# The seven products of w_out: one weight sum on VectorE, another order of the products, gated transfers of x, factors made earlier

## The chip, the cores and the metric

The kernel runs on one core of a Trainium2 chip. Its engines are TensorE (PE; its weight loads are shown as PEld), VectorE (DVE), ScalarE (ACT), GpSimd (POOL) and SyncE (SP); each works through its own instructions in order, and they meet through semaphores. SP and POOL also issue transfers (DMA) between the chip's main memory (DRAM) and the on-chip memory (SBUF); all transfers share the core's 16 DMA engines. The metric is the device time of one execution in microseconds.

## What is computed

One layer of a hybrid encoder over 512 tokens and 2048 features. After the input projection, attention and the gating unit, two branches are merged, projected by `w_out` and added to `x`; then comes a squared-ReLU MLP:

```python
merged = jax.nn.sigmoid(gate_a) * y_a + jax.nn.sigmoid(gate_b) * y_b
x = x + merged @ w_out[l]

h2 = rms_norm(x, g_ff[l])
x = x + jnp.square(jax.nn.relu(h2 @ w_ff1[l])) @ w_ff2[l]
```

The change concerns `x + merged @ w_out[l]`: 512 x 2048 times 2048 x 2048, in float32.

## The kernel before

**Exact products from split factors.** PE multiplies a rounded float32 form, so each factor is split: `hi` is the rounded copy (made on ACT, line 113) and `lo` the rest (made on DVE, line 114). One product then takes three matmuls (`mm3`, lines 72 to 74): hi x hi, hi x lo, lo x hi.

**Seven products instead of eight.** The large projections use Strassen's scheme in Winograd's form: a 2 x 2 block product with seven block multiplications, named y11, y21, m7, m6, y22, m4 and m5. Each needs a weight factor (a weight block or a sum of blocks) and an activation factor. Class `Sums` (line 168) makes the weight factors of one 2 x 2 set of blocks, w11, w12, w21, w22, in six tiles of 128 x 1024 numbers (512 KB): four for the blocks, one (`a`) for m7's factor, one (`c`) for m6's and then y22's. `Sums.loads` gives SP the loads; `Sums.parts(name)` makes the sum that the product needs and splits it into hi and lo. In w_out the sums are made in two ways:

- by a transfer that adds to what is in SBUF (issued by POOL, `accum_op=ALU.add`): m7's factor (`given`: `a` is loaded with one block by SP and the other is added by line 321), m5's (line 192, issued at m7), y22's (line 205, issued right after m6's factor has been split: block (1, 0) is added to `c`);
- by an addition on DVE: m6's (line 194).

**The stage of w_out.** Lines 940 to 966 call `strassen_tokens` four times: `f` is the half of the 2048 rows of `w_out`, `g` the half of its columns, in the order (0, 0), (0, 1), (1, 0), (1, 1). A call makes two `Sums` (`i`, each of 4 x 128 rows) and then, product by product, multiplies: 2 `Sums` x 2 token tiles x 2 row blocks x 3 = 24 matmuls of 128 x 512. The order of the products is `NAMES` (line 159), and another one in the last call (`last`, line 324). When a product is done, `evac_x` adds it from PSUM to the result tiles `x2[token tile, column block]`; `takes` (line 901) says to which and with what sign, and `done` (line 904) with which product a tile is complete. Complete tiles are written to DRAM (`kept`, line 952), squared for the next norm and scaled (lines 954 and 955).

**x itself** is added by transfers too: in the calls (0, 1) and (1, 0), `between_x` (line 957) issues after each product one or two accumulating transfers (256 KB, on POOL) into the `x2` tiles of the other column half. Their only condition is that the tile's own last addition is done.

**The activation factors** are kept in `ms`: `split_merged` makes y11, y21 and y22, `merged_factors` makes m7, m6, m4 and m5, each with a subtraction or an addition on DVE (line 255), a copy on ACT and a subtraction on DVE. For the row half `f` = 0 they are indices 0 to 3, for `f` = 1 indices 4 to 7. When they are made is written out by hand: `steps` (lines 828 to 870) is a list of tasks by step, where a step is a piece of a projection (in w_oa and w_ob) or a product (in w_out); step `OB` = 16 is the first of w_ob, `XO` = 32 the first product of w_out, `FF` = 60 the first piece of the MLP.

**What sets the order.** The instructions of an engine are put in order when the kernel is built, by a planner that goes by dependencies, by the order in the program and by a simulation of times; an instruction can stand in its queue ahead of another that the program names first. `tc.issue_after(ins)` puts the issues in its block behind `ins` on that engine. Tiles come from pools: `slots` has 64 tiles of 128 x 512, the weight tiles two pools of six, the split weights (`w_piece`) six, which is three pairs of hi and lo. A tile that is asked for again waits for its last reader.

Of the kernel before, what the change touches and what calls it, by code (L numbers as in the profile page):

```python
# [13 lines left out]
ALU = mybir.AluOpType  # L14
AX = mybir.AxisListType

P = 128
# [11 lines left out]
W = 512  # L29
# [6 lines left out]
def tile_hybrid_layer(ctx: ExitStack, tc: tile.TileContext, x, g_mix, w_in, g_q, g_k, ln_g, ln_b,  # L36
# [4 lines left out]
    nc = tc.nc  # L41
# [21 lines left out]
    def tiny(n, name):  # L63
        return small.tile([P, n], F32, name=name, tag=f"tiny{n}")
# [103 lines left out]
    class Sums:  # L168


        def __init__(self, blocks, tiles, loaded=True, twice=False, given=False):


            self.blocks, self.loaded, self.twice, self.given = blocks, loaded, twice, given
            self.w11, self.w12, self.w21, self.w22, self.a, self.c = tiles
            self.take = {"y11": self.w11, "y21": self.w12, "m7": self.a, "m6": self.c, "y22": self.c,
                         "m4": self.w22, "m5": self.w21}

        def loads(self):
            order = [(self.w11, (0, 0)), (self.w12, (1, 0)), (self.w21, (0, 1)), (self.w22, (1, 1))]  # L180
            if self.given:
                order.insert(2, (self.a, (0, 0)))
            for t, hc in order:
                self.load = state["load"] = nc.sync.dma_start(out=t, in_=self.blocks[hc])
                yield

        def parts(self, name):
            if name == "m7":
                if not self.given:
                    nc.vector.tensor_tensor(out=self.a, in0=self.w11, in1=self.w21, op=ALU.add)  # L190
                if self.loaded:
                    state["sum"] = nc.gpsimd.dma_start(out=self.w21, in_=self.blocks[1, 1], accum_op=ALU.add)  # L192
            if name == "m6":
                nc.vector.tensor_tensor(out=self.c, in0=self.a, in1=self.w22, op=ALU.add)  # L194
            if name == "y22" and not self.twice:
                nc.vector.tensor_tensor(out=self.c, in0=self.c, in1=self.w12, op=ALU.add)
            if name == "m5" and not self.loaded:
                nc.vector.tensor_tensor(out=self.w21, in0=self.w21, in1=self.w22, op=ALU.add)
            src = self.take[name]
            hi, lo = piece("w_hi"), piece("w_lo")  # L200
            like = "p (k c) -> p k c"
            hi, lo = (t.rearrange(like, k=src.shape[1]) for t in (hi, lo))
            split_to(hi, lo, src)
            if name == "m6" and self.twice:
                state["sum"] = nc.gpsimd.dma_start(out=self.c, in_=self.blocks[1, 0], accum_op=ALU.add)
            return hi, lo
# [97 lines left out]

    SIGNS = (1.0, -1.0)

    def strassen_tokens(wap, r0, c0, lhs, evac, between, loaded=True, after=None, last=False, by_dma=False):

        KQ = 2
        ws = []  # L310
        for i in range(2):
            rows = wap[r0 + i * 2 * KQ * P:r0 + (i + 1) * 2 * KQ * P, :]
            blocks = {(h, c): rows[:, c0 + c * W:c0 + (c + 1) * W].rearrange("(k h p) c -> h p k c", p=P, h=2)[h]
                      for h in range(2) for c in range(2)}
            pool = (state["raw"], state["more"])[i]
            ws.append(Sums(blocks, [pool.tile([P, KQ, W], F32, name="w_raw", tag="w_raw") for _ in range(6)],
                           loaded, by_dma, by_dma))
        collections.deque(zip(*[w.loads() for w in ws]), 0)
        if by_dma:
            for w in ws:  # L320
                nc.gpsimd.dma_start(out=w.a, in_=w.blocks[0, 1], accum_op=ALU.add)
        state["loads"] = [w.load for w in ws]
        banks = {}
        names = ("y11", "m7", "m6", "m5", "y22", "m4", "y21") if last else NAMES
        for name in names:
            b, new = BANK[name]
            if new:
                banks[b] = [(aux if b in (1, 3) else acc)("q") for _ in range(2)]
            factors = []
            turns = [(i, t) for i in range(2) for t in range(2)]  # L330
            if last and name == names[-1]:
                turns.sort(key=lambda it: it[1])
            for i, t in turns:
                if i == len(factors):
                    with tc.issue_after(after.ins) if after and name == "m7" else nullcontext():
                        factors.append(ws[i].parts(name))
                hi, lo = factors[i]
                for k in range(KQ):
                    y = [part[:, t * P:(t + 1) * P] for part in lhs[name][i * KQ + k]]
                    mm3(banks[b][t], y, (hi[:, k, :], lo[:, k, :]), new and i == 0 and k == 0,  # L340
                        i == 1 and k == KQ - 1, skip_group_check=True)
            for t in range(2):
                evac(name, t, banks[b][t])
            between(name)
            step()
# [26 lines left out]
    mhalf = const.tile([P, 4], F32, name="mhalf")  # L372
# [258 lines left out]
    wsT, ws, bs = [], [], []  # L631
# [61 lines left out]
    for half in range(2):  # L693
# [4 lines left out]
        if half:  # L698
            steps = collections.defaultdict(list)
# [52 lines left out]
    order = gate_pairs[:1]  # L752
# [10 lines left out]
    for i, item in enumerate(order):  # L763
# [6 lines left out]
        else:  # L770
            c0, n, func = item
# [56 lines left out]
    steps = collections.defaultdict(list)  # L828
# [10 lines left out]
    def split_merged(k, names=("y11", "y21", "y22")):  # L839
        for name in names:  # L840
            half = int(name[2]) - 1
            ms[name, k] = halves(mt[2 * k + int(name[1]) - 1][:, half * HS:(half + 1) * HS])

    def merged_factors(k, *names):
        for name in names:
            factor(ms, mt[2 * k:2 * k + 2], k, name)

    OB, XO, FF = 16, 32, 60
    for i in range(2):
        n, a, b = OB + 4 * (i + 1), 2 * i, 2 * i + 1  # L850
        for at, f in enumerate([lambda a=a: split_merged(a),
# [1 line left out]
                                lambda a=a, b=b: (merged_factors(a, "m4", "m5"), merged_factors(b, "m7")),  # L853
                                lambda b=b: merged_factors(b, "m6", "m4", "m5")]):
            steps[n + at].append(f)
    for i in range(2):
        steps[OB + 14 + i].append(lambda i=i: split_merged(4 + i, ("y11", "y21")))
    steps[XO].append(lambda: [split_merged(4 + i, ("y22",)) for i in range(2)])
    for i in range(2):
        steps[XO + 1 + i].append(lambda i=i: split_merged(6 + i))  # L860
        for n, name in ((7, "m6"), (10, "m4"), (15, "m5")):
            steps[XO + n + i].append(lambda i=i, name=name: [merged_factors(4 + 2 * i + c, name) for c in range(2)])
    for i in range(4):
        steps[XO + 3 + i].append(lambda i=i: merged_factors(4 + i, "m7"))
    for n, what in ((21, (0, 0)), (22, (0, 1)), (23, (1, 0)), (24, (1, 1)), (25, (3, 1)), (26, (2, 1)), (27, (3, 0)),
                    (27, (2, 0))):
        steps[XO + n].append(lambda what=what: turned(*what))
# [29 lines left out]
    x2, x2T, hs = {}, {}, {}  # L897
# [29 lines left out]
            factor(hs, act, k, name, -1.0 if name in ("m7", "m4") else None, pool)  # L927

    CHUNK = 4

    class Merged:

# [7 lines left out]
    for f in range(2):  # L940
        for g in range(2):
            def evac_x(name, t, o):
                for half, c, op in takes[name]:
                    key = 2 * half + t, 2 * g + c
                    if key not in x2:
                        x2[key] = slot("x2")
                        nc.scalar.activation(out=x2[key], in_=o, func=AF.Copy, scale=1.0 if op == ALU.add else -1.0)
                    else:
                        nc.vector.tensor_tensor(out=x2[key], in0=x2[key], in1=o, op=op)
                for half, c in done[g].get(name, []) if f else []:  # L950
                    tb, j = 2 * half + t, 2 * g + c
                    nc.sync.dma_start(out=kept[tb, j], in_=x2[tb, j])
                    xs = x2s[tb, j] = slot("xs")
                    nc.scalar.activation(out=xs, in_=x2[tb, j], func=AF.Square, accum_out=ss2[:, tb, j:j + 1])
                    nc.scalar.activation(out=xs, in_=x2[tb, j], func=AF.Copy, scale=rstd[:, tb:tb + 1])

            def between_x(name):
                if f != g:
                    i = NAMES.index(name)
                    for n in (i, len(NAMES)) if i == len(NAMES) - 1 else (i,):  # L960
                        tb, j = n % NTB, 2 * (1 - g) + n // NTB
                        nc.gpsimd.dma_start(out=x2[tb, j], in_=x[tb * P:(tb + 1) * P, j * W:(j + 1) * W],
                                            accum_op=ALU.add)

            strassen_tokens(w_out[0], f * CHUNK * 2 * P, g * 2 * W, Merged(f), evac_x, between_x, last=f == 1 and g == 1,
                            by_dma=True)
    second.close()
    third = ExitStack()
    long = third.enter_context(tc.tile_pool(name="long2", bufs=LONG))
# [81 lines left out]
    for p in range(PLAIN):  # L1051
        o = plain_pair(w_ff1[0], p * 2 * P, hs, "f1", (0, 4, 8, 12) if p else (0, 4, 12, 8))
        act = []
        for c in range(2):
            t = slot("relu")
# [122 lines left out]
```

## Time and profile before

| | us |
|---|---|
| median of 3 runs | 2431.47 |
| lowest, highest | 2430.99, 2433.60 |
| the profiled execution | 2433.7 |
| its span | 2432.0 |
| PE busy in it | 2392.4 |
| DVE busy | 1943.6 |
| ACT busy | 1339.1 |
| POOL busy | 519.4 |

The profile is one execution, recorded by the chip. Its views give busy times by engine, groups of instructions by source line, who waited for whom, the chain of work that ended last, and the instructions in order of time. Times in the views are us from the start of the span. An engine's row names the line of the kernel, the operation, the tile written, the tiles read, and in brackets how long the engine stood idle before and what released it. The stage of w_out lies between about 985 and 1180 us. w_ob comes before it; the first projection of the MLP (matmuls written to `f`) begins at 1170.5 us, while the last products still run.

### The profile page before, as it was taken

Reading aid. Unit: us, or ns where it says so; the run is one execution under the profiler, and the core shown is the slowest. Engines: PE = TensorE matmul, PEld = TensorE weight load, DVE = VectorE, ACT = ScalarE, POOL = GpSimd, SP = SyncE. Lnnn points to the kernel's source line nnn. Section 1 sums busy time; section 2 is a strip of 40 time slices with the busy share of each in tenths; the row PEclk is TensorE's granted clock in tenths of the full one; section 3 lists DMA queues with packets and bytes.
Section 4 is the critical chain, followed back from the end, with each engine's and each line's share of the span. In section 5 each row is a group of like instructions: output and inputs, shape, how many; then the busy total and the mean of one; then the engine's idle time right before and its main releaser. Section 6 shows DMA issues by size and latency. Waiting matters only on the chain.

```text
span 2432.0 us, 34714 instructions
## 1 busy us (share of the span) xinstructions
PE 2392.4 (98%) x12436; PEld 2050.1 (84%) x12436; DVE 1943.6 (80%) x2662; ACT 1339.1 (55%) x2094; POOL 519.4 (21%) x625
## 2 busy tenths in 40 slices
PE   9999999999999999988999999999999999999999
PEld 7888888888888888766988888888888888888887
DVE  4576887777878558656879988888888998989987
ACT  5345666666666223446767777777775443333333
POOL 0101322222223333221000000000014434322210
PEclk9999999999999999999999999999999999999999
DMA  5557888888888855697469888888887999867753
GB/s 175 198 159 161 170 176 175 187 168 183 172 183 195 324 189 166 154 215 193 122 183 247 225 223 227 232 234 239 224 248 282 317 283 316 260 213 208 239 180 98
DMA packets 517389, 507.23 MB, mean 209 GB/s; under 512 B 21152, under 2 KB 399072, under 8 KB 517216
## 3 DMA queue, kind: packets, MB, share of 16 engines
q1 hardware_dynamic: 383056, 336.68, 43.4%
q0 software_dynamic: 133872, 167.80, 33.4%
q8 instruction: 98, 1.61, 0.3%
q10 hardware_dynamic: 288, 0.52, 0.1%
q14 instruction: 75, 0.61, 0.1%
HBM read 414.22 MB, written 89.65 MB: 207 GB/s over the span
## 4 chain that ended last, share of the span: by engine, by line
PE 92%; DMA 3%; DVE 2%; ACT 1%; issue 1%; POOL 0%; SPq 0%; DVEq 0%; ACTq 0%; POOLq 0%
PE q L227 17%; PE fork L227 13%; PE q L72 9%; PE q L73 9%; PE q L74 9%; PE q L230 9%; PE fork L230 7%; DMA w_raw<-in_w_out_dram 2%; PE v L72 1%; PE v L73 1%; PE v L74 1%; PE vg L74 1%; PE vg L73 1%; PE yb L74 1%; PE yb L72 1%; PE vg L72 1%
## 5 line engine op out<-in xcount | busy, mean ns | idle before, releaser
L113 ACT CAST w_hi<-w_raw 128x1024 fp32r<-128x1024 f32 (+1 forms) x688 | 722.5, 1051 | 809.8 <-PE q L73 366.8
L114 DVE TENSOR_TENSOR w_lo<-w_raw,w_hi 128x1024 fp32r<-128x1024 f32 (+1 forms) x688 | 838.0, 1220 | 245.7 <-ACT w_hi L113 227.7
L73 PE MATMUL q<-w_lo,ys 128*128 128x512 f32 x1120 | 439.5, 392 | 0.9 <-DVE w_lo L114 0.8
L74 PE MATMUL q<-w_hi,ys 128*128 128x512 f32 x1120 | 437.4, 391 | 0.0
L72 PE MATMUL q<-w_hi,ys 128*128 128x512 f32 x1120 | 395.1, 392 | 24.5 <-ACT w_hi L113 23.5
L227 PE MATMUL q<-ys,w_hi 128*128 128x512 f32 x1632 | 411.0, 394 | 4.4 <-ACT fork L235 4.4
L227 PEld LDWEIGHTS q<-ys,w_hi 128*128 128x128 f32 x1632 | 293.6, 189 | 58.3 <-ACT fork L235 5.2
L72 PEld LDWEIGHTS q<-w_hi,ys 128*128 128x128 f32 x1120 | 211.1, 189 | 70.0 <-ACT w_hi L113 24.7
L73 PEld LDWEIGHTS q<-w_lo,ys 128*128 128x128 f32 x1120 | 211.4, 189 | 48.8 <-DVE w_lo L114 5.3
L74 PEld LDWEIGHTS q<-w_hi,ys 128*128 128x128 f32 x1120 | 211.4, 189 | 43.5
L227 PE MATMUL fork<-ys,w_hi 128*128 128x512 f32 x944 | 236.2, 392 | 0.0
L230 PEld LDWEIGHTS q<-ys,w_lo 128*128 128x128 f32 x1632 | 221.2, 190 | 14.4 <-DVE w_lo L114 0.3
L192 POOL DMA_DIRECT2D w_raw<-in_w_ff_dram x57 | 79.2, 1390 | 714.3 <-ACT act L1009 162.1
L230 PE MATMUL q<-ys,w_lo 128*128 128x256 f32 x1632 | 228.1, 282 | 0.1
L227 PEld LDWEIGHTS fork<-ys,w_hi 128*128 128x128 f32 x944 | 171.3, 189 | 31.6
L1071 POOL DMA_DIRECT2D ys<-store x224 | 126.3, 586 | 180.2 <-PE q L74 112.1
L101 DVE TENSOR_TENSOR w_lo<-w_raw,w_hi 128x1024 fp32r<-128x1024 f32 x71 | 93.5, 1317 | 67.9 <-ACT w_hi L99 66.1
L99 ACT CAST w_hi<-w_raw 128x1024 fp32r<-128x1024 f32 x71 | 74.6, 1051 | 119.8 <-issue 43.7
L230 PEld LDWEIGHTS fork<-ys,w_lo 128*128 128x128 f32 x944 | 128.8, 190 | 9.2
L1120 DVE SCALAR_TENSOR_TENSOR total<-q,plus,total 128x512 f32<-128x512 f32 x180 | 132.1, 745 | 4.2 <-PE q L74 4.1
L190 DVE TENSOR_TENSOR w_raw<-w_raw 128x1024 f32<-128x1024 f32 x90 | 110.0, 1223 | 31.1 <-DMA w_raw<-in_w_in_dram 11.3
L194 DVE TENSOR_TENSOR w_raw<-w_raw 128x1024 f32<-128x1024 f32 x98 | 119.9, 1223 | 18.0 <-DMA w_raw<-in_w_out_dram 11.0
(264 smaller groups left out, 3680.9 us busy)
## 6 DMA issues: line engine op xcount, KB each, us to landing
w_raw<-in_w_ff_dram SPq DMA_DIRECT2D x256, 512.0 KB, 5.5
w_raw<-in_w_in_dram SPq DMA_DIRECT2D x143, 512.0 KB, 5.3
ys<-store POOLq DMA_DIRECT2D x224, 256.0 KB, 6.7
w_raw<-in_w_ff_dram POOLq DMA_DIRECT2D x57, 512.0 KB, 6.8
w_raw<-in_w_in_dram POOLq DMA_DIRECT2D x56, 512.0 KB, 6.5
store<-ys_hi SPq DMA_DIRECT2D x90, 256.0 KB, 5.1
store<-ys_lo SPq DMA_DIRECT2D x90, 256.0 KB, 5.1
w_raw<-in_w_out_dram SPq DMA_DIRECT2D x40, 512.0 KB, 5.0
```

What stands on the lines that cost most here:

```text
L72: nc.tensor.matmul(o, lhsT=lh[0], rhs=rh[0], start=start, stop=False, **kw)
L73: nc.tensor.matmul(o, lhsT=lh[0], rhs=rh[1], start=False, stop=False, **kw)
L74: nc.tensor.matmul(o, lhsT=lh[1], rhs=rh[0], start=False, stop=stop, **kw)
L101: nc.vector.tensor_tensor(out=lo, in0=raw, in1=f32(hi), op=ALU.subtract)
L113: nc.scalar.copy(out=hi, in_=src)
L114: state["lo"] = nc.vector.tensor_tensor(out=lo, in0=src, in1=f32(hi), op=ALU.subtract)
L190: nc.vector.tensor_tensor(out=self.a, in0=self.w11, in1=self.w21, op=ALU.add)
L194: nc.vector.tensor_tensor(out=self.c, in0=self.a, in1=self.w22, op=ALU.add)
L227: nc.tensor.matmul(o, lhsT=hi[:, k, :], rhs=rhs[name][k], start=name in ("y11", "m7") and k == 0, stop=False, skip_group_check=True)
L230: nc.tensor.matmul(o[:, :HS], lhsT=lo[:, k, :], rhs=rhs[name][k][:, :HS], start=False, stop=k == KH - 1, skip_group_check=True)
L1071: nc.gpsimd.dma_start(out=f32(t), in_=store[f][HELD.index(name), p])
L1120: nc.vector.scalar_tensor_tensor(out=a, in0=o, scalar=part, in1=a, op0=ALU.mult, op1=ALU.add)
```

## The change

Four things are changed, all of them about w_out.

1. The way `given` goes. m7's factor is made by an addition on DVE, w11 + w21, as in the other projections; `a` is loaded no more, and the accumulating transfers of line 321 are gone. The flag that stays, `twice`, still leaves y22's sum to a transfer.
2. In the first three calls the order of the products is y11, y21, m7, m6, m4, m5, y22. The tile that y22 and m5 share is now complete with y22 (`ready` in place of `done`).
3. x's transfers in the calls (0, 1) and (1, 0) get a gate: a POOL instruction that reads a few columns of the `x2` tile which the product at hand has just been added to. The transfers are issued behind it.
4. The activation factors for `f` = 1 are made at other steps; `split_merged` of indices 4 and 5, with y22, and their m7 come in w_ob's last steps.

```diff
-        def __init__(self, blocks, tiles, loaded=True, twice=False, given=False):
+        def __init__(self, blocks, tiles, loaded=True, twice=False):
...
         def loads(self):
-            order = [(self.w11, (0, 0)), (self.w12, (1, 0)), (self.w21, (0, 1)), (self.w22, (1, 1))]
-            if self.given:
-                order.insert(2, (self.a, (0, 0)))
-            for t, hc in order:
+            for t, hc in ((self.w11, (0, 0)), (self.w12, (1, 0)), (self.w21, (0, 1)), (self.w22, (1, 1))):
...
             if name == "m7":
-                if not self.given:
-                    nc.vector.tensor_tensor(out=self.a, in0=self.w11, in1=self.w21, op=ALU.add)
+                nc.vector.tensor_tensor(out=self.a, in0=self.w11, in1=self.w21, op=ALU.add)
...
-                           loaded, by_dma, by_dma))
+                           loaded, twice))
         collections.deque(zip(*[w.loads() for w in ws]), 0)
-        if by_dma:
-            for w in ws:
-                nc.gpsimd.dma_start(out=w.a, in_=w.blocks[0, 1], accum_op=ALU.add)
...
         names = ("y11", "m7", "m6", "m5", "y22", "m4", "y21") if last else NAMES
+        if twice and not last:
+            names = ("y11", "y21", "m7", "m6", "m4", "m5", "y22")
...
-    for i in range(2):
-        steps[OB + 14 + i].append(lambda i=i: split_merged(4 + i, ("y11", "y21")))
-    steps[XO].append(lambda: [split_merged(4 + i, ("y22",)) for i in range(2)])
-    for i in range(2):
-        steps[XO + 1 + i].append(lambda i=i: split_merged(6 + i))
-        for n, name in ((7, "m6"), (10, "m4"), (15, "m5")):
-            steps[XO + n + i].append(lambda i=i, name=name: [merged_factors(4 + 2 * i + c, name) for c in range(2)])
-    for i in range(4):
-        steps[XO + 3 + i].append(lambda i=i: merged_factors(4 + i, "m7"))
+    for n, f in ((-3, lambda: split_merged(4)), (-2, lambda: split_merged(5)),
+                 (-1, lambda: [merged_factors(k, "m7") for k in (4, 5)]),
+                 (0, lambda: split_merged(6)), (1, lambda: split_merged(7)),
+                 (2, lambda: merged_factors(6, "m7")), (3, lambda: merged_factors(7, "m7")),
+                 (4, lambda: merged_factors(4, "m6")), (5, lambda: merged_factors(5, "m6")),
+                 (7, lambda: [merged_factors(k, "m6") for k in (6, 7)]),
+                 (9, lambda: [merged_factors(k, "m4") for k in (4, 5)]),
+                 (10, lambda: [merged_factors(k, "m4") for k in (6, 7)]),
+                 (14, lambda: [merged_factors(k, "m5") for k in (4, 5)]),
+                 (15, lambda: [merged_factors(k, "m5") for k in (6, 7)])):
+        steps[XO + n].append(f)
...
+    ready = ({"y21": [(0, 0)], "m4": [(0, 1)], "m5": [(1, 1)], "y22": [(1, 0)]}, done[1])
...
-                for half, c in done[g].get(name, []) if f else []:
+                for half, c in ready[g].get(name, []) if f else []:
...
                 if f != g:
+                    half, c, _ = takes[name][0]
+                    gate = nc.gpsimd.tensor_tensor(out=tiny(4, "gate"), in0=x2[2 * half + 1, 2 * g + c][:, :4],
+                                                   in1=mhalf, op=ALU.mult)
                     i = NAMES.index(name)
                     for n in (i, len(NAMES)) if i == len(NAMES) - 1 else (i,):
                         tb, j = n % NTB, 2 * (1 - g) + n // NTB
-                        nc.gpsimd.dma_start(out=x2[tb, j], in_=x[tb * P:(tb + 1) * P, j * W:(j + 1) * W],
-                                            accum_op=ALU.add)
+                        with tc.issue_after(gate.ins):
+                            nc.gpsimd.dma_start(out=x2[tb, j], in_=x[tb * P:(tb + 1) * P, j * W:(j + 1) * W],
+                                                accum_op=ALU.add)
```

More of the change, by code (lines that the diff above doesn't have):

```diff
@@ L168, in tile_hybrid_layer @@
     class Sums:
-        def __init__(self, blocks, tiles, loaded=True, twice=False, given=False):
-            self.blocks, self.loaded, self.twice, self.given = blocks, loaded, twice, given
+        def __init__(self, blocks, tiles, loaded=True, twice=False):
+            self.blocks, self.loaded, self.twice = blocks, loaded, twice
             self.w11, self.w12, self.w21, self.w22, self.a, self.c = tiles
@@ L305, in tile_hybrid_layer, with strassen_tokens @@
     SIGNS = (1.0, -1.0)
-    def strassen_tokens(wap, r0, c0, lhs, evac, between, loaded=True, after=None, last=False, by_dma=False):
+    def strassen_tokens(wap, r0, c0, lhs, evac, between, loaded=True, after=None, last=False, twice=False):
         KQ = 2
@@ L961, in between_x @@
                         tb, j = n % NTB, 2 * (1 - g) + n // NTB
-                        nc.gpsimd.dma_start(out=x2[tb, j], in_=x[tb * P:(tb + 1) * P, j * W:(j + 1) * W],
-                                            accum_op=ALU.add)
+                        with tc.issue_after(gate.ins):
+                            nc.gpsimd.dma_start(out=x2[tb, j], in_=x[tb * P:(tb + 1) * P, j * W:(j + 1) * W],
+                                                accum_op=ALU.add)
             strassen_tokens(w_out[0], f * CHUNK * 2 * P, g * 2 * W, Merged(f), evac_x, between_x, last=f == 1 and g == 1,
-                            by_dma=True)
+                            twice=True)
     second.close()
```

## The prediction

> **What bounds the kernel now.** I read the page first. The chain that ended last is PE work nearly all the way, but one transfer has a share of its own, and it belongs to a single stage:
>
> ```profile
> PE 92%; DMA 3%; DVE 2%; ACT 1%; issue 1%; POOL 0%; SPq 0%; DVEq 0%; ACTq 0%; POOLq 0%
> ```
>
> So I asked who waited for whom between 935 and 1215 us, which holds the w_out stage, and for PE in that stage.
>
> ```profile
> ACT w_hi L113 <- DMA w_raw<-in_w_out_dram: 41.0, 6, 15.2
> POOL w_raw L321 <- DMA w_raw<-in_w_out_dram: 11.7, 1, 11.7
> PEld q L72 <- ACT w_hi L113: 24.7, 3, 11.9
> PE q L72 <- ACT w_hi L113: 23.5, 3, 11.5
> PEld q L73 <- DVE w_lo L114: 2.7, 6, 0.8
> ```
>
> The columns are total us, times, longest. PE stands still three times, waiting for a w_hi whose copy on ACT waits for a transfer. The timeline of PE places the three stalls; first comes the start of the stage and the last matmul before each stall.
>
> ```profile
> 984.92 0.39 PE L72 MATMUL q<-w_hi,ys 128*128 128x512 f32 x1
> 1006.46 0.39 PE L74 MATMUL q<-w_hi,ys 128*128 128x512 f32 x1
> 1010.58 1.22 PE L72 MATMUL q<-w_hi,ys 128*128 128x512 f32 x2 [3.74 <-ACT w_hi L113]
> ...
> 1052.10 0.39 PE L74 MATMUL q<-w_hi,ys 128*128 128x512 f32 x1
> 1063.94 1.22 PE L72 MATMUL q<-w_hi,ys 128*128 128x512 f32 x2 [11.45 <-ACT w_hi L113]
> ...
> 1103.90 0.39 PE L74 MATMUL q<-w_hi,ys 128*128 128x512 f32 x1
> 1112.57 1.22 PE L72 MATMUL q<-w_hi,ys 128*128 128x512 f32 x2 [8.29 <-ACT w_hi L113]
> ```
>
> One product is 2 x 2 x 2 x 3 = 24 matmuls. From 984.92 to 1006.46 lie 95 steps, if four products (96 matmuls) ran: 0.2267 us a matmul, 5.44 us a product. So the first stall stands behind the fourth product, m6, and the fifth is y22. Seven products later (38.1 us) comes the next stall, again ahead of y22, and so the third. The fourth stage, whose order is another one, has none. What y22 waits for is in the chain, in order of time:
>
> ```profile
> 999.77 9.64 DMA w_raw<-in_w_out_dram
> 1051.39 11.38 DMA w_raw<-in_w_out_dram
> 1101.59 9.81 DMA w_raw<-in_w_out_dram
> 1012.64 0.43 PE q L74
> 1018.57 0.23 PE q L74
> ```
>
> These start at POOL's issues of line 205, the accumulating transfer that makes y22's weight sum out of m6's: issued when m6's weights have been split, landed 10 us later, wanted at once. The two PE rows show the second price: after a stall matmuls go at 0.43 us, then at 0.23 again.
>
> **The change part by part.** *y22 moved behind m4 and m5 in three stages.* It removes the stalls if the transfer lands within two products more, 10.88 us. Their size, from the starts above plus 0.23 for the last matmul: 1010.58 - 1006.69 = 3.89, 1063.94 - 1052.33 = 11.61, 1112.57 - 1104.13 = 8.44, together 23.94 us. The slow clock behind them: from 1010.58 to 1052.33 are 41.75 us for 168 matmuls worth 38.09, loss 3.66; from 1063.94 to 1104.13, 40.19, loss 2.10. Behind the third:
>
> ```profile
> 1113.60 1.05 PE L912 MATMUL x2T<-ident,xs 128*128 128x128 f32 x4
> 1117.23 1.07 PE L72 MATMUL q<-w_hi,ys 128*128 128x512 f32 x4
> ```
>
> 1112.57 to 1117.23 is 4.66 us for 12 matmuls (2.72) and four transposes (about 0.13 each at full clock, an estimate from half their 0.26): loss 1.4. Sum 7.16, and with the stalls **31.1 us**.
>
> In a sentence of its own: the Trainium skill (TensorE: Matmul & The Clock Gate, The HAM clock gate) says that an idle window of about 3.4 us halves PE's clock and that as long a busy one restores it; the trace agrees (0.43 against 0.23), and an estimate by it, 1.7 us for each stall, would make the sum 23.9 + 5.1 = 29.0 instead of 31.1.
>
> Is y22's transfer in time? In the second stage m6's last split and the transfer's issue stood so:
>
> ```profile
> 1045.23 1.22 DVE L114 TENSOR_TENSOR w_lo<-w_raw,w_hi 128x1024 fp32r<-128x1024 f32 x1 [0.54 <-ACT w_hi L113]
> 1048.85 1.20 POOL L321 DMA_DIRECT2D w_raw<-in_w_out_dram x1 [11.70 <-DMA w_raw<-in_w_out_dram]
> 1051.39 4.21 POOL L205 DMA_DIRECT2D w_raw<-in_w_out_dram x2
> ```
>
> The split ended at 1046.5, but POOL held a line 321 of the next stage, 11.70 us long, in front of line 205. That instruction is gone after the change, so the issue can come some 4 us sooner. Even at 1047.5 with the worst landing, 11.4, it is there at 1058.9; y22 would start at 1052.33 + 10.88 = 1063.2, and its first copy and split (1.05 + 1.22) can start as late as 1060.9. In the third stage the transfer lands at 1101.59 + 9.81 = 1111.4 with no sooner issue, against 1104.13 + 10.88 - 2.27 = 1112.7: slack 1.3 us without help. This is the thin place.
>
> *m7's sum on VectorE.* Away go 8 loads on SP (0.37 us of its time each) and 8 accumulating issues on POOL (1.20 us), 16 x 512 KB of traffic. DMA is the resource that is full here; the stages, one window each:
>
> ```profile
> core 0: us, PE busy (x) PEld busy (x) DVE busy (x) ACT busy (x) POOL busy (x), PEclk, DMA share, GB/s
> 984.92:1030.60 45.68, 41.90 (x171) 33.23 (x170) 28.34 (x44) 22.46 (x35) 14.30 (x13) 0.93 0.74 173
> 1030.60:1082.40 51.80, 40.31 (x169) 32.22 (x168) 28.65 (x38) 21.36 (x31) 14.69 (x15) 0.90 0.92 208
> 1082.40:1131.30 48.90, 40.61 (x177) 33.25 (x176) 29.91 (x37) 19.10 (x29) 10.81 (x10) 0.93 0.89 215
> 1131.30:1170.50 39.20, 38.16 (x185) 30.72 (x183) 35.23 (x58) 36.65 (x77) 2.41 (x2) 1.00 0.59 172
> ...
> q1 hardware_dynamic: 383056, 336.68, 43.4%
> q0 software_dynamic: 133872, 167.80, 33.4%
> ```
>
> The first three stages hold 33.8 + 47.7 + 43.5 = 125 us of full DMA time, more than three stall-free stages, 114.3 us. Over the span q1 moved 336.68 MB in 43.4% of 2432 us, 319 GB/s; q0 207. Six loads and six accumulations fall in these stages (the first pair came earlier): 3.15 MB each, 9.9 + 15.2 = 25 us. About 100 of 114 us remain: full, no longer over.
>
> Added: eight DVE sums. Line 190 is the same operation elsewhere:
>
> ```profile
> L190 DVE TENSOR_TENSOR w_raw<-w_raw 128x1024 f32<-128x1024 f32 x90 | 110.0, 1223 | 31.1 <-DMA w_raw<-in_w_in_dram 11.3
> ```
>
> 2.45 us a stage. DVE would have 28.3 + 2.4 of 38.1, then 31.1, 32.4 and 37.7 of 39.2: room in all, little in the fourth. Bounds for PE: 0 to 8 x 1.22 = 9.8 us, and below zero by the 2.7 us that it now waits for w_lo. The nearest row is that wait, 0.45 us a time; one more a stage: **1.8 us**. The sum reads w21, so w11's buffer comes free two products later, at m7; its next load has until product 7, some 22 us, with 5.0 us to land; in the fourth stage m7 is second, and w21, freed by m5's split, has about 2.4 products, 13 us. Taken as 0.
>
> *x's transfers gated.* 14 gates of a few columns, then the 16 transfers that are there now. The same operation and a transfer stand so:
>
> ```profile
> x<-in_x_dram POOLq DMA_DIRECT2D x16, 256.0 KB, 7.5
> 935.36 0.32 POOL L822 TENSOR_TENSOR gate<-w_lo,mhalf 128x4 f32<-128x4 f32 x1 [9.80 <-DVE w_lo L101]
> 997.61 2.27 POOL L962 DMA_DIRECT2D x<-in_x_dram x2
> ```
>
> Today two x transfers go out at 997.61, just ahead of y22's at 999.77; gated, they wait a stage. Behind a waiting gate on POOL stand lines 192 and 205, for which m5 and y22 wait. In program order a product's accumulation stands ahead of its own gate, so a gate costs line 205 only the wait for m7's results, about one evacuation of 0.7 us after m6 begins. 0 on the path, by y22's two products of cover; without them, the stalls above again. Bounds: a gain up to the 3.9 us of the first stall (counted already), a loss in the rivals. The last x tile leaves after y22 in the third stage and is wanted by m6 of the fourth, three products (16 us) later against 7.5 us: 0.
>
> In a sentence of its own, against the change: the Trainium skill (SBUF — State Buffer, Who interferes with whom) says that a VectorE instruction with two SBUF inputs and a GpSimd instruction that reads SBUF block each other, and no row here shows it; by it 14 gates of 0.32 us would hold DVE for 4.5 us at most, an estimate, and if all fell on PE the sum would be smaller by that.
>
> *Factors earlier.* The same instructions, moved: of the second half's factors, y22 of two k and m7 of two k are now made under w_ob. That is two splits and two factors with splits, about 6 x 0.42 us of DVE; the cover is w_ob's stage, where PE never waits:
>
> ```profile
> 938.00:984.90 46.90, 46.90 (x208) 38.86 (x207) 36.06 (x47) 14.43 (x27) 17.40 (x16) 1.00 0.47 136
> ```
>
> 36.1 of 46.9 us busy, so 0; if the cover were gone, 2.5 us. By my count of live tiles the slots go to 64 of 64 at most there while sT's come free, so a short wait is possible.
>
> **Sum:** 31.1 - 1.8 = 29.3 us. The profiled execution took 2433.7 us (span 2432.0), so 2404.4 for its like; the median, 2431.47, lies 2.2 lower: **2402 us**.
>
> **The rivals.** *A: y22 is late in its new place too.* For it: 1.3 us of slack in the third stage, and x and line 192 still share the queue; the longest landing of any w_raw transfer is 13.4 us:
>
> ```profile
> DMA to landing us min/median/max: 3.1/6.2/13.4
> ```
>
> Against: fewer transfers, y22's issue no longer behind line 321. Price: 13.4 - 9.8 - 1.3 = 2.3 us and a slow clock of 2.1 to 3.7, in two stages: 9 to 12, so 2411 to 2414. Chance 0.12. *B: DMA stays the bound.* If the removed transfers free nothing because the rest is what is slow, 125 us stand against 114.3: 10.7 us and ramps, 2413 to 2420. Against: the rates above. Chance 0.05. *C: nothing gained*, the stall changes place (m5 waits for line 192, say, for as long): 2427 to 2436, chance 0.03. *D, slower: gates stand in front of the accumulations.* POOL runs in order. If the built order puts line 205 behind m5's gate and line 192 behind m4's, y22 waits for m5's evacuation plus a landing, about 13 us and 3 of slow clock, m5 for about 9 and 3, in the two gated stages: 2402 + 56 = 2458; from line 205 alone 2434, which counts with C. It decides from the point where line 205 starts later than about 10 us before y22. For it: the trace's POOL order is not program order (line 321 runs a stage ahead). Against: that order runs ahead where data are ready, and a split is ready before an evacuation. Chance 0.06.
>
> **How the numbers follow.** The forecast, 2398 to 2410, gets 0.74. Its low end is every stall and the w_lo waits gone: 2431.5 - 31.1 - 2.7 = 2397.7. Its high end is the whole DVE bound: 9.8 us in place of 1.8. The range, **2398 to 2412**, takes in the near half of A: about 0.8. A measurement of this kernel tells about 0.2%, 4.9 us, from no change. Faster: forecast, A and B, 0.91. Same: C, 0.03. Slower: D, 0.06.
>
> **What would show it.** Right: PE's waits for w_hi in w_out gone, each of the four stages 38 to 40 us, the granted clock 1.0 throughout, DMA share under 0.9; line 205 issued within some 3 us of m6's second split; no line 321. The DVE term: PE's waits for w_lo there, now 2.7 us, up by no more than 2. Wrong: a PE wait ahead of y22 or m5 with a transfer behind it (A or D, told apart by whether line 205 started late or landed late), or a DVE that is never idle in the fourth stage.

## The result, and the profile after

| | before | after |
|---|---|---|
| median, us | 2432.53 | 2399.06 |
| lowest, highest of 4 runs | 2430.99, 2435.43 | 2397.43, 2400.23 |
| the profiled execution | 2433.7 | 2400.23 |
| its span | 2432.0 | 2398.5 |

The changed kernel takes 0.9861 of the time before (95% interval 0.9843 to 0.9878): 33.5 us less, where 29.3 were forecast.

The page of the changed kernel, shares of the chain of work that ended last by engine. No transfer has a share above 1% any more:

```profile
PE 96%; DMA 1%; DVE 1%; ACT 1%; issue 0%; POOL 0%; SPq 0%; DVEq 0%; ACTq 0%; POOLq 0%
```

Who waited for whom between 935 and 1215 us in the changed kernel: all that PE's weight loads still wait for (us in total, times, longest). Both are matmuls of the MLP's `f`; the rows of w_out, 24.7 and 2.7 us before, are gone:

```profile
PEld f L74 <- DVE w_lo L101: 0.8, 1, 0.8
PEld f L72 <- ACT w_hi L99: 0.3, 1, 0.3
```

Stretches of the changed kernel's w_out, one for each call, columns as in the prediction's table (PE, PEld, DVE, ACT, POOL busy, granted clock, DMA share, GB/s). The first begins with PE's first matmul of w_out, at 981.99, and the last ends with the first matmul of `f`. PE is busy all but all of the time and at full clock; the first three stages last 38 to 39 us instead of 46 to 52:

```profile
981.99:1020.07 38.08, 38.08 (x169) 31.56 (x168) 31.34 (x43) 22.03 (x32) 8.73 (x7) 1.00 0.58 139
1020.07:1058.15 38.08, 38.08 (x169) 31.56 (x168) 29.88 (x38) 21.45 (x30) 15.33 (x17) 1.00 0.89 206
1058.15:1096.71 38.56, 38.56 (x173) 31.95 (x172) 32.16 (x38) 22.80 (x35) 14.15 (x19) 1.00 1.03 256
1096.71:1134.63 37.92, 37.89 (x189) 31.38 (x187) 32.66 (x54) 33.23 (x68) 4.41 (x4) 1.00 0.66 176
```

The transfer that PE had waited for, y22's (line 205 before, 201 after). First the kernel before, then the changed one; for the six issues in the first three calls of each, minimum, median and maximum of the time from issue to landing:

```profile
DMA to landing us min/median/max: 9.6/11.5/13.2
```

```profile
DMA to landing us min/median/max: 5.6/6.9/8.7
```

It lands in 0.6 of the time. The prediction had put the whole gain down to the order of the products and had left the landing at 10 to 11 us. That asks which of the four edits did it.

How much was gained by the end of w_out, and how much of it arrived: the matmuls of `f` that follow w_out (line 72; minimum, median, maximum in ns, then start of the first and of the last), first before, then after.

```profile
L72 PE MATMUL f<-ys,w_hi x128: 280/283/388, 1170.5 to 1224.6; 128*128 128x256 f32 x128
```

```profile
L72 PE MATMUL f<-ys,w_hi x128: 280/283/388, 1134.6 to 1188.7; 128*128 128x256 f32 x128
```

The gain is 35.9 us at both ends of the row, but not all of it was made in w_out. PE's first matmul of w_out starts at 984.92 before, as the prediction's rows show, and after at

```profile
981.99 0.39 PE L72 MATMUL q<-w_hi,ys 128*128 128x512 f32 x1
```

So 2.9 us were there already. They come from the first 13 us of the kernel, which no edit touches: in the profiled execution of the kernel before, PE waited for a transfer of x, and its next matmuls started 0.43 us apart in place of 0.23. The rows of that place, before and then after:

```profile
9.26 0.80 PE L449 MATMUL xT<-ident,xk 128*128 128x128 f32 x4 [2.00 <-DMA xk<-in_x_dram]
```

```profile
7.86 0.63 PE L444 MATMUL xT<-ident,xk 128*128 128x128 f32 x4 [0.28 <-DMA xk<-in_x_dram]
```

In the profiles of the other twelve kernels below, too, w_out starts at 981.8 to 982.5. How often the kernel before loses these 2.9 us is not known, since one execution of it was profiled. From the first matmul of w_out to the first of `f` are 185.6 us before and 152.6 after: w_out itself gained 32.9 us.

At the end of the span the gain is 33.5: 2.4 us are given back later in the MLP. What stands in the chain there, before and then after:

```profile
1898.28 7.94 DMA store<-ys
1908.32 12.24 DMA w_raw<-in_w_ff_dram
```

```profile
1862.11 10.54 DMA store<-ys
1874.76 12.31 DMA w_raw<-in_w_ff_dram
```

The store took 2.6 us longer in this execution, the load behind it as long as before; the change touches neither. From the last start in the row of `f` to the end of the span are 1207.4 us before and 1209.8 after; in two kernels of the experiments below, whose MLP is the same, they are 1206.4 (`e8_order_and_sum`, where the store took 8.93 us) and 1211.1 (`e9_l321_behind`). So 2.4 us lie within what this part varies by. Whether the order built or the execution makes the difference was not settled.

### The profile page after: what moved, and what is told of

Read it like the earlier page. It is cut to its first block, busy times and chain, and to the rows that moved or that the text cites. A ratio compares the mean times of both kernels' runs of the same rounds, so it can differ in the third digit from the quotient of the medians.

```text
span 2398.5 us, 34712 instructions
## 1 busy us (share of the span) xinstructions
PE 2382.6 (99%) x12436; PEld 2046.4 (85%) x12436; DVE 1948.1 (81%) x2670; ACT 1340.2 (56%) x2094; POOL 516.6 (22%) x631
## 4 chain that ended last, share of the span: by engine, by line
PE 96%; DMA 1%; DVE 1%; ACT 1%; issue 0%; POOL 0%; SPq 0%; DVEq 0%; ACTq 0%; POOLq 0%
PE q L223 18%; PE fork L223 13%; PE q L73 10%; PE q L74 10%; PE q L72 10%; PE q L226 9%; PE fork L226 7%; PE v L72 1%; PE v L74 1%; PE v L73 1%; PE vg L72 1%; PE vg L74 1%; PE yb L72 1%; PE yb L74 1%; PE yb L73 1%; PE vg L73 1%
## 5 line engine op out<-in xcount | busy, mean ns | idle before, releaser
L186 DVE TENSOR_TENSOR w_raw<-w_raw 128x1024 f32<-128x1024 f32 x98 | 119.7, 1222 | 39.2 <-DMA w_raw<-in_w_in_dram 10.6
L101 DVE TENSOR_TENSOR w_lo<-w_raw,w_hi 128x1024 fp32r<-128x1024 f32 x71 | 87.7, 1237 | 61.7 <-ACT w_hi L99 59.9
L226 PE MATMUL fork<-ys,w_lo 128*128 128x256 f32 x944 | 131.7, 283 | 0.0
```

Source lines behind the costliest of these rows:

```text
L101: nc.vector.tensor_tensor(out=lo, in0=raw, in1=f32(hi), op=ALU.subtract)
L226: nc.tensor.matmul(o[:, :HS], lhsT=lo[:, k, :], rhs=rhs[name][k][:, :HS], start=False, stop=k == KH - 1, skip_group_check=True)
```

## The experiments

The change has four parts: **order** (y22 last), **sum** (m7's weight sum on DVE instead of by transfers), **gates** (x's transfers) and **factors** (steps of the second half's activation factors). The comparisons with the kernel before are medians of 4 runs (e7 of 10, e12 of 5; the kernel before, run beside them each time, took 2431.7 to 2432.3 us), with 95% intervals of the ratio.

| | order | sum | gates | factors | other | us | ratio |
|---|---|---|---|---|---|---|---|
| after | x | x | x | x | | 2399.06 | 0.9861 [0.9843, 0.9878] |
| e1_old_order | | x | x | x | | 2402.65 | 0.9880 [0.9865, 0.9895] |
| e2_m7_by_dma | x | | x | x | | 2403.06 | 0.9884 [0.9869, 0.9899] |
| e3_no_gates | x | x | | x | | 2397.28 | 0.9857 [0.9841, 0.9874] |
| e4_old_factors | x | x | x | | | 2398.88 | 0.9864 [0.9849, 0.9878] |
| e5_order_alone | x | | | | | 2410.06 | 0.9908 [0.9893, 0.9923] |
| e6_sum_alone | | x | | | | 2409.23 | 0.9908 [0.9892, 0.9925] |
| e7_gates_alone | | | x | x | | 2428.77 | 0.9983 [0.9974, 0.9993] |
| e8_order_and_sum | x | x | | | | 2398.42 | 0.9862 [0.9847, 0.9877] |
| e9_l321_behind | | | | | line 321 behind 205 | 2411.31 | 0.9915 [0.9898, 0.9931] |
| e10_sum_thrice | x | x | x | x | the sums thrice | 2399.51 | 0.9868 [0.9853, 0.9882] |
| e11_sum_and_gates | | x | x | | | 2408.16 | 0.9905 [0.9890, 0.9920] |
| e12_order_and_queue | x | | | | line 321 behind 205 | 2410.92 | 0.9919 [0.9905, 0.9933] |

### One part undone: the first four

Theory 1 is the prediction's: the new order carries the gain, and the sum costs a little. Theory 2: the traffic that the sum takes away carries it. Each run is the changed kernel with one part as it was before.

**e1_old_order** takes the new order back:

```diff
-        if twice and not last:
-            names = ("y11", "y21", "m7", "m6", "m4", "m5", "y22")
...
-                for half, c in ready[g].get(name, []) if f else []:
+                for half, c in done[g].get(name, []) if f else []:
```

> The changed kernel with the old order of products in the first three calls (y22 right behind m6); all else as changed. Theory 1 (the order carries the gain: y22's transfer takes about 10 us to land and is wanted at once): three stalls ahead of y22 come back. The transfer can be issued when m6's second split ends, some 6 us before y22 would start, so about 4 to 6 us each and 2 to 3 of slow clock: 15 to 27 us over the changed kernel's 2399, so 2414 to 2426. Theory 2 (the load on the DMA engines carried it, and 8.4 MB less are moved): the transfer now lands in about 5 us, no stall worth naming: 2399 to 2403.

**e2_m7_by_dma** takes the sum back: `a` is loaded by SP, and POOL issues the accumulating transfers again.

```diff
+            if self.given:
+                order.insert(2, (self.a, (0, 0)))
...
+        if twice:
+            for w in ws:
+                nc.gpsimd.dma_start(out=w.a, in_=w.blocks[0, 1], accum_op=ALU.add)
```

> The changed kernel with m7's weight sum made by a transfer again (8 loads and 8 accumulating transfers come back, 8 additions on DVE go). Theory 1 (order): y22 has two products of cover, so the stalls stay away; 2397 to 2403. Theory 2 (DMA load): 125 us of DMA time must fit into 114 us of stages and POOL's line for m7 stands in front of y22's transfer again: 2410 to 2420.

**e3_no_gates** issues x's transfers without a gate:

```diff
-                    gate = nc.gpsimd.tensor_tensor(out=tiny(4, "gate"), in0=x2[2 * half + 1, 2 * g + c][:, :4],
-                                                   in1=mhalf, op=ALU.mult)
...
-                        with tc.issue_after(gate.ins):
```

> The changed kernel without the gates on x's transfers. Prediction's step (gates cost and bring nothing once y22 has its cover): 2397 to 2402, no wait of PE for a transfer in w_out. Rival (the gates keep x's 16 transfers out of the way of line 201's and line 188's): x again goes out ahead of y22's transfer in the first call, stalls of 2 to 5 us with slow clock: 2404 to 2412.

**e4_old_factors** puts the second half's factors back to the steps where they were:

```diff
-    for n, f in ((-3, lambda: split_merged(4)), (-2, lambda: split_merged(5)),
...
+    for i in range(2):
+        steps[OB + 14 + i].append(lambda i=i: split_merged(4 + i, ("y11", "y21")))
...
```

> The changed kernel with the old steps for the second half's activation factors. Prediction's step (no effect, the same work beside other work): 2397 to 2402, PE without a wait in w_out. Rival (DVE has 31.9 of 38.1 us in the first call; with 2 to 3 us more it becomes late there): PE waits for w_lo or evacuations in the first call, 2402 to 2406.

Measured: 2402.65, 2403.06, 2397.28 and 2398.88 us. Gates and factors can be left out one at a time, and what moves (1.8 and 0.2 us) is not told from nothing. The other two were a surprise: without the order nearly all of the gain stays, against theory 1, and without the sum too, against theory 2. The waits of PE's weight loads in e1, and those of ACT for w_out's transfers in e1:

```profile
PEld q L72 <- ACT w_hi L113: 2.7, 2, 2.2
...
ACT w_hi L113 <- DMA w_raw<-in_w_out_dram: 16.9, 6, 6.6
```

In the old order, where y22 follows m6 at once, PE waits 2.7 us in place of 24.7 and ACT 16.9 in place of 41.0; y22's transfer lands in 5.7 to 9.0 us. In e2 it lands late, but the two products of cover take most of it:

```profile
PEld q L73 <- DVE w_lo L114: 3.8, 3, 3.0
PEld q L72 <- ACT w_hi L113: 3.1, 3, 1.5
...
DMA to landing us min/median/max: 8.3/14.1/17.4
```

### One part alone

From this theory 3: order and sum are two cures of one stall, one by time for the transfer and the other by making it quick; either alone gives most, and the gains don't add. The rival is that gates or factors had carried the rest in e1 and e2. Three kernels make one part alone on the kernel before (the edits as above, turned round), and one makes the two parts without the others. e7, named after the gates, has the new factor steps as well.

> The kernel before with the new order of products alone (and `ready`, which goes with it); m7's sum by transfer, no gates, old factor steps. Theory 3 (two causes, either cure is nearly enough: m7's transfers make y22's land in 11 to 13 us where it takes 7 without them, and the order gives 10.9 us of cover): line 205 still lands in 11 us or more, PE's waits small, 2400 to 2410. Rival (theory 2, DMA load alone decides): 2412 or more.

> The kernel before with m7's sum on DVE alone; old order, no gates, old factor steps. Theory 3: line 201 lands in about 7 us, issued about 7 us before y22's copy is due, PE's waits small: 2400 to 2408. Rival (theory 1, the order alone decides): three stalls of 4 to 6 us and slow clock, 2414 or more. The first run (e1) spoke against it, but had the gates; without them x's transfers go out ahead of y22's in the first call.

> The kernel before with the gates on x's transfers and the new factor steps; old order, m7's sum by transfer. Theory 3 (neither cure is there): line 205 stays behind line 321 and lands in 11 us; the first call's stall shrinks as x's two transfers are gone from it: 2418 to 2432. Rival (the gates do their share of the gain by moving x): 2410 or less.

> The changed kernel without gates and with the old factor steps, so the new order and m7's sum on DVE alone. Theory 3: all of the gain is in these two, 2396 to 2399, the level of the run without gates (2397.3) or of the changed kernel (2399.1). Rival (the gates or the early factors bring something that only shows when both are gone): 2400 or more, with PE waits for w_lo in the first call.

Measured: 2410.06, 2409.23, 2428.77 and 2398.42 us. Order alone gains 22 us, the sum alone 23, both 33.7: all that the whole change gains. Gates and factors alone gain 0.17%, 3 to 4 us. e5 shows why the order alone is not enough. Its waits of PE's weight loads, a row of POOL's timeline, and the landing of line 205 in the first three calls:

```profile
PEld q L72 <- ACT w_hi L113: 5.9, 3, 4.6
```

```profile
1037.61 1.20 POOL L321 DMA_DIRECT2D w_raw<-in_w_out_dram x1 [11.63 <-DMA w_raw<-in_w_out_dram]
```

```profile
DMA to landing us min/median/max: 9.0/12.7/20.3
```

Line 321, the next call's m7 sum, still blocks POOL for 11.63 us, and one of y22's transfers, issued behind it in that call, needs 20.3 us, 9.4 more than the cover of 10.88; the longest wait that is left is 4.6 us. In e6 line 321 is gone, the landing is 5.7 to 10.8 us, and what is left is the missing cover:

```profile
PEld q L72 <- ACT w_hi L113: 8.1, 3, 4.1
```

In e7 most of the stalls is there:

```profile
PEld q L72 <- ACT w_hi L113: 18.9, 4, 8.8
```

### The traffic, or the place in the queue?

The sum removes line 321 from POOL's queue, where it waits and then goes out just ahead of line 205, and it takes away 25 us of DMA time as well, by the prediction's estimate. **e9_l321_behind** keeps every transfer of the kernel before, and all else of it, and only makes POOL issue line 321 behind line 205:

```diff
         if by_dma:
-            for w in ws:
-                nc.gpsimd.dma_start(out=w.a, in_=w.blocks[0, 1], accum_op=ALU.add)
+            with tc.issue_after(state["sum"].ins):
+                for w in ws:
+                    nc.gpsimd.dma_start(out=w.a, in_=w.blocks[0, 1], accum_op=ALU.add)
```

> The kernel before, with one thing changed: line 321's transfers are issued behind line 205's on POOL. Same bytes, same products, same order of them. Theory 3 as refined by the runs so far (the landing under load decides, POOL's order does a part): line 205 starts up to 4 us sooner in the second and third call and lands in 10 us or more as before; 2422 to 2430. Rival (line 321 in front of line 205 is the main cause): the stalls shrink to the size of the run with m7's sum on DVE alone, 2408 to 2414.

Measured: 2411.31 us. Without one byte less, 21 us of the 33.5 are there. My theory at that point was that it would do little; the rival, the place in the queue, was right. POOL's timeline of e9 in the second call (lines from 321 on are one higher) and the landing of line 205 in the first three calls:

```profile
1038.79 1.49 POOL L205 DMA_DIRECT2D w_raw<-in_w_out_dram x1
1040.81 1.20 POOL L205 DMA_DIRECT2D w_raw<-in_w_out_dram x1 [0.53 <-DVE w_lo L114]
1041.54 2.93 POOL L322 DMA_DIRECT2D w_raw<-in_w_out_dram x2
```

```profile
DMA to landing us min/median/max: 6.0/8.2/9.4
```

Beside the prediction's rows of the same place (line 321 idle for 11.70 us until 1048.85, line 205 at 1051.39): both issues of line 205 now go out by 1040.81, the second as soon as the split that frees `c` has ended, and the median landing is 8.2 instead of 11.5 us. So the transfer was late twice over: its issue stood some 5 us behind m6's last split (1046.5 to 1051.39), and of the 10 to 11 us that the prediction took for its own duration some 3 were what went out in front of it.

**e12_order_and_queue** adds the new order to e9 (edits as in e9 and, turned round, in e1). Theory 4: the queue is all, so the DVE sum isn't needed and this reaches the changed kernel. Rival: the traffic that stays costs something.

> The kernel before with the new order of products and line 321's transfers behind line 205's; m7's sum stays with the transfers, no gates, old factor steps. Against the run with the new order alone (2410) and the one with order and DVE sum (2398.4). Theory 4 (y22's transfer was late because line 321 stood in front of it, not because 8.4 MB more are moved): 2397 to 2402, no wait of PE in the first three calls. Rival (the bytes still cost, 250 GB/s and more in the third call): PE waits for w_hi or for m5's transfer, 2403 to 2409.

Measured: 2410.92 us, no better than e9; theory 4 fell, and the loss is larger than the rival gave. The landings of e12 in the first three calls, line 205's and then line 322's; then waits for weights, PE's and DVE's:

```profile
DMA to landing us min/median/max: 6.0/8.0/9.8
...
DMA to landing us min/median/max: 10.8/13.5/16.3
```

```profile
PEld q L73 <- DVE w_lo L114: 9.4, 5, 3.4
...
DVE w_raw L194 <- DMA w_raw<-in_w_out_dram: 20.5, 6, 7.0
```

y22's transfer is quick here and no w_hi of it is waited for. The next call's weights are late instead: DVE, which works in order, stands in m6's sum (line 194) until they land. The same row of the kernel before:

```profile
DVE w_raw L194 <- DMA w_raw<-in_w_out_dram: 7.9, 6, 2.5
```

The splits behind that sum are late with it, as DVE's timeline of e12 shows:

```profile
1060.21 1.23 DVE L194 TENSOR_TENSOR w_raw<-w_raw 128x1024 f32<-128x1024 f32 x1 [7.05 <-DMA w_raw<-in_w_out_dram]
1061.36 1.22 DVE L114 TENSOR_TENSOR w_lo<-w_raw,w_hi 128x1024 fp32r<-128x1024 f32 x1
```

The transfer that this sum waited for is a load on SP, not line 322, which had been issued by 1041.3 and had landed. It is a row of the chain:

```profile
1047.75 12.34 DMA w_raw<-in_w_out_dram
```

In e8 the load that the same sum needs goes out here, and lands within 7.1 us:

```profile
1038.96 0.37 SPq L181 DMA_DIRECT2D w_raw<-in_w_out_dram x1
...
DMA to landing us min/median/max: 7.1/7.1/7.1
```

The second call of e12 itself runs only 2.0 us behind that of e8, so its load goes out some 7 us later and then takes 5.2 us longer. With `a` loaded too, SP issues ten loads a call instead of eight. In both kernels this one goes out as a split ends and frees its tile, at 1047.7 in e12 and 1038.9 in e8.

So m7's sum by transfer does have a price, once the queue is mended: 12.5 us between e12 (2410.92) and e8 (2398.42), which differ only in who makes m7's sum. In the old order the same difference is 2.1 us (e9 against e6). Whether the bytes make the price or the later issue of the loads was not separated: no run moves `a`'s load behind the others. The sum on DVE brings both cures at once: a free queue, and loads that are neither late nor slow.

### What the DVE sum costs, and what the factors do

**e10_sum_thrice** makes m7's addition three times over in w_out, into the same tile:

```diff
-                nc.vector.tensor_tensor(out=self.a, in0=self.w11, in1=self.w21, op=ALU.add)
+                for _ in range(3 if self.twice and state.get("out") else 1):
+                    nc.vector.tensor_tensor(out=self.a, in0=self.w11, in1=self.w21, op=ALU.add)
...
+        state["out"] = twice
```

> The changed kernel with m7's addition on DVE made three times in w_out (16 more of 1.22 us, 4.9 us a call; the result is the same). It measures the cover of the sum, for which the prediction charged 1.8 us and the runs show 0. If DVE has slack ahead of m7: 2397 to 2401 and no wait of PE for w_lo in the first three calls. Rival (DVE is near its limit): PE waits for w_lo or w_hi by up to 4 us a call, 2403 to 2415.

Measured: 2399.51 us, level with the changed kernel. 16 additions more, some 19.5 us of DVE at the 1.22 us of the prediction's row, cost PE 1.5 us of waits:

```profile
PEld q L73 <- DVE w_lo L114: 1.5, 4, 0.7
```

One addition is free, then, not by a narrow margin.

**e11_sum_and_gates** is e1 with the old factor steps. It should tell what made e1 6.6 us faster than e6: the gates (my theory) or the factors (the rival).

> m7's sum on DVE and the gates on x's transfers, with the old order and the old factor steps. With the new steps it took 2402.7, and the sum without gates and new steps 2409.2. Theory (the gates keep x out of the way of y22's transfer, which matters only where y22 wants it at once): 2401 to 2405. Rival (it was the factor steps): 2407 to 2411.

Measured: 2408.16 us. It was the factors: in the old order their new steps are worth 5.5 us (2408.16 to 2402.65), the gates 1.1 (2409.23 to 2408.16), which isn't told from nothing. POOL's issues of line 201 in the second and third calls, in e11 and then in e1:

```profile
1036.84 2.43 POOL L201 DMA_DIRECT2D w_raw<-in_w_out_dram x2 [0.32 <-issue]
...
1076.40 1.20 POOL L201 DMA_DIRECT2D w_raw<-in_w_out_dram x1 [0.23 <-DVE w_lo L114]
```

```profile
1035.07 1.20 POOL L201 DMA_DIRECT2D w_raw<-in_w_out_dram x1 [1.11 <-issue]
...
1073.50 1.20 POOL L201 DMA_DIRECT2D w_raw<-in_w_out_dram x1 [0.23 <-issue]
```

With the new steps the issue is 1.8 and 2.9 us sooner, of which 0.7 is a later start of w_out in e11's profiled execution (982.54 against 981.84). That fits: DVE has less to do ahead of m6's split, and the old order hands such a delay on to PE while the new one has cover for it (e4 against the changed kernel: 0). That reason is argued from the issue times, not shown by a run of its own.

## Why the prediction was right, step by step

**The stalls ahead of y22 and the slow clock behind them, 31.1 us: right.** All three are gone, and with them the clock's dips (1.00 in every stage). From the first matmul of w_out to the first of `f` 32.9 us are gained, 1.8 more than the terms hold. Two small waits of the fourth call that they left out are in PE's timeline of the kernel before:

```profile
1140.58 0.55 PE L912 MATMUL x2T<-ident,xs 128*128 128x128 f32 x3 [0.19 <-ACT xs L955]
...
1152.00 0.50 PE L72 MATMUL q<-w_hi,ys 128*128 128x512 f32 x1 [0.81 <-DVE x L949]
```

They make 1.0 us; the other 0.8 is not assigned. On the clock, the prediction gave beside its 31.1 a 29.0 by the rule in the Trainium skill (TensorE: Matmul & The Clock Gate, The HAM clock gate). The outcome lies above both, so it does not tell them apart. In the trace of the kernel before, matmuls start 0.43 us apart until 1016.3, 1067.5 and 1115.3, that is for 5.7, 3.6 and 2.7 us behind the three stalls: the halved rate agrees with the rule, the one length of 3.4 us that the prediction took from it does not.

**"y22 moved behind m4 and m5 … removes the stalls if the transfer lands within two products more": right only in company.** The prediction booked the whole gain here. Alone (e5) the order gains 22 us, since with line 321 still there one landing took 20.3 us. The prediction named that help, "y22's issue no longer behind line 321", but as 4 us of margin; e9 shows that it is a cure by itself, worth 21 us. The assumption that failed is the landing, 9.6 to 11.4 us as the transfer's own price: it is 5.6 to 8.7 in the changed kernel, and 6.0 to 9.4 in e9 with every byte still moved. The "thin place", 1.3 us of slack in the third stage, is not thin in the changed kernel, and in e5, where PE did wait for a w_hi of y22, it was in the second stage.

**m7's sum, a cost of 1.8 us: wrong in sign and place.** Its cost is 0 (no w_lo wait of PE in w_out after, 1.5 us even with three times the additions), the near end of the bounds 0 to 9.8. And it is a cure of its own: alone it gains 23 us. DVE in the last stage, for which 37.7 of 39.2 us were forecast, is busy for 32.7 of 37.9; the sums for that call are made between 1082 and 1095, before its stretch begins.

**DMA full, no longer over: right, with one sign missed.** 0.58 x 38.1 + 0.89 x 38.1 + 1.03 x 38.6 = 96 us of DMA time in the three stages, about 100 forecast. The third stage stands at 1.03 where under 0.9 had been named, and PE waited for nothing there: a full stage need not be a stall.

**Gates 0, factors 0: right** for this kernel (e3, e4, and e8 without either). Line 201 goes out right behind m6's split, so gates don't stand in front of it, as rival D needed:

```profile
1036.25 1.20 POOL L201 DMA_DIRECT2D w_raw<-in_w_out_dram x1 [0.46 <-DVE w_lo L114]
```

Rivals A to C are out as well: no PE wait ahead of y22 or of m5, and no stage bound by DMA. The total came out 2.9 us lower than forecast. In w_out 1.8 were uncounted and 1.8 of DVE were not paid; 2.9 were gained at the start of the kernel and 2.4 lost in the MLP, which the change did not make; and 1.3 go off for the base: the median before is 1.1 higher in this comparison than the one that the forecast started from, and 0.2 is rounding. These parts are read from one profiled execution of each kernel. That the parts outside w_out nearly cancel is luck.

## What to carry to other kernels

Before a slow transfer's landing time is taken as its price, look at what the same queue issued just ahead of it, and what that had been waiting for: moving an early transfer of the next stage behind the urgent one gained 21 of 33.5 us here without removing a byte. When two edits relieve the same wait, neither their gains alone nor their losses when undone add up to the whole (22 and 23 alone, 33.7 together, 3.6 and 4.0 when undone), so parts are to be tried alone and undone. A gain is measured from the first to the last instruction of the stage that was changed, not from the start of the span, where two executions can differ already (2.9 us here). Work moved onto an engine with slack can be priced by doing it three times.

## What the hardware showed that I had not expected

Ten of the 14 gates, 128 x 4 numbers on POOL, take 0.74 to 1.20 us where 0.32 had been assumed and 0.19 is enough. Their row in the changed kernel (minimum, median, maximum in ns), and some of them in POOL's timeline; then DVE's timeline at the same places:

```profile
L958 POOL TENSOR_TENSOR gate<-x,mhalf x14: 188/739/1197, 1027.6 to 1097.9; 128x4 f32<-128x4 f32 x14
```

```profile
1027.57 0.74 POOL L958 TENSOR_TENSOR gate<-x,mhalf 128x4 f32<-128x4 f32 x1 [14.09 <-ACT x L945]
...
1070.08 0.19 POOL L958 TENSOR_TENSOR gate<-x,mhalf 128x4 f32<-128x4 f32 x1 [4.17 <-DVE x L947]
...
1092.66 0.19 POOL L958 TENSOR_TENSOR gate<-x,mhalf 128x4 f32<-128x4 f32 x1 [3.39 <-DVE x L947]
```

```profile
1027.02 1.23 DVE L114 TENSOR_TENSOR w_lo<-w_raw,w_hi 128x1024 fp32r<-128x1024 f32 x1 [1.95 <-ACT w_hi L113]
...
1070.09 1.26 DVE L114 TENSOR_TENSOR w_lo<-w_raw,w_hi 128x1024 fp32r<-128x1024 f32 x1
...
1090.69 2.47 DVE L947 TENSOR_TENSOR x<-x,q 128x512 f32<-128x512 f32 x4
```

The first gate shown starts while a split with two SBUF inputs runs on DVE, and it ends with it: 1028.31 against 1028.25. All ten slow gates lie so, each beside a DVE instruction with two SBUF inputs. The second one shown starts 0.01 us ahead of the split, takes 0.19 us, and the split takes 1.26 in place of 1.22. The third runs beside additions of line 947, which read one tile from SBUF and one from PSUM, and takes 0.19 as well. This is the exclusive lock of the Trainium skill (SBUF — State Buffer, Who interferes with whom), of which the prediction could show no row. The prediction's estimate went the other way about, though: it had DVE held, and here it is nearly always POOL. Without the gates (e3) the kernel is 1.8 us faster, which is not told from nothing.
